# Depthwise convolution of 31 taps: the running sum moved to a PSUM bank, eight taps per tile moved to ScalarE and GpSimd

## The chip, the cores and the metric

The kernel runs on one core of one Trainium2 chip. The metric is the device time of one execution in microseconds (us), measured without the profiler; beside it stands one profiled execution, which the trace describes.

## The reference, cut to what matters

Two transformer blocks in sequence on 512 tokens of 1024 features, in float32. The change lies in the first block, between its first and second feed-forward layers:

```python
u = modulate(x, sh2, sc2)
proj = u @ w_in
xr, gr, conf_in, gate_a, gate_b = jnp.split(proj, IN_SPLITS, axis=-1)

xr = causal_depthwise_conv(xr, rnn_conv_w, rnn_conv_b)          # 4 taps
hr = rg_lru(xr, rglru_w_r, rglru_b_r, rglru_w_i, rglru_b_i, rglru_lambda)
ya = (hr * jax.nn.gelu(gr)) @ rnn_w_proj

glu = conf_in[..., :D_CONV] * jax.nn.sigmoid(conf_in[..., D_CONV:])
hb = causal_depthwise_conv(glu, conf_dw_w, conf_dw_b)           # 31 taps
hb = jax.nn.silu(layer_norm(hb, conf_ln_g, conf_ln_b))
yb = hb @ conf_w_proj

merged = jax.nn.sigmoid(gate_a) * ya + jax.nn.sigmoid(gate_b) * yb
out = merged @ mix_w_out
```

The convolution of 31 taps works on each feature by itself, along the tokens, and looks only backwards. The second block has, among other layers, an attention with a decay (retention), which is named below because it shares a pool of banks.

## The kernel before, in words

Activations lie feature-major: a tile is 128 features by 512 tokens, and eight tiles (KT = 8) make 1024 features. A matrix product of 1024 by 1024 is eight jobs, one for each tile of the result. A job has eight pairs of tiles, and each pair takes three matmuls of 128x512, since values and weights are each split in a high part and a low remainder (`passes`): 24 matmuls that add up in one PSUM bank from the pool `ps`. The weight of a job comes by a DMA that SyncE issues (`wr`, four buffers); ScalarE rounds it to the high part (`wh`, three buffers), and VectorE subtracts to get the low part (`wl`, three buffers). `ft(..., evac, pump)` lays down one job and, behind it, the evacuation of its bank.

PSUM has eight banks of 128x512. `ps` has six of them and `st` two; `st` is for transposes and broadcasts of column statistics.

Work that belongs to no job goes on a list: `later(cost, f)` appends a piece with a cost, and `pump(budget)` takes pieces off the list as jobs are laid down, until their costs use up the budget of the job. `delay(jobs, f)` runs a piece some jobs later, and `settle` empties both lists. The scheduler of the framework then fixes an order for each engine, which the engine keeps; an engine that waits holds up all that stands behind it in its order.

`middle` holds the stage: 16 jobs for the two halves of `conf_in` (`ev_b`, `ev_a`), 16 for `xr` and `gr` with the recurrence behind them, eight each for the two gates, eight of `rnn_w_proj`, then `settle`, eight of `conf_w_proj` and eight of `mix_w_out`. Each `ev_a` makes a tile `g` and puts 30 taps of it on the list; a tap is one VectorE instruction, `hb = g shifted * w + hb`, in place in SBUF. Behind the last tap of a tile follow its sums for the layer norm (`conf_add`), behind the last tile's the column sums by eight transposes (`column_sums`, L280), the power on GpSimd (`rsqrt`, L284), the broadcast by eight more (`diag_bcast`, L273), and then `conf_apply` for each tile: VectorE's corrections, SiLU on ScalarE, the split. The jobs of `conf_w_proj` read what `conf_apply` makes.

Line numbers of the profile that come up below: L133 is any two-operand VectorE or GpSimd operation, L136 any scalar_tensor_tensor (the taps among them, `s<-s,ccw,s`), L147 any ScalarE activation without a bias tile, L152 any matmul of a job.

In the retention of the second block, `ev_g` multiplies a gate job's bank by a tile on VectorE, `scores(h)` takes four banks of `ps` for one head, and the next gate job follows.

Of the kernel before, what the change touches and what calls it, by code (L numbers as in the profile page):

```python
# [9 lines left out]
F32 = mybir.dt.float32  # L10
F32R = mybir.dt.float32r
I32 = mybir.dt.int32
AF = mybir.ActivationFunctionType
ALU = mybir.AluOpType
AX = mybir.AxisListType

S = 512
# [40 lines left out]
class Net:  # L58
    def __init__(self, ctx, tc, a, out):
        self.tc, self.nc, self.a, self.out = tc, tc.nc, a, out  # L60
        pool = lambda **k: ctx.enter_context(tc.tile_pool(**k))
        self.const = pool(name="const", bufs=1)
        self.sl = pool(name="sl", bufs=1)
        self.wr = pool(name="wr", bufs=4)
        self.wh = pool(name="wh", bufs=3)
        self.wl = pool(name="wl", bufs=3)
        self.ps = pool(name="ps", bufs=6, space=bass.MemoryType.PSUM)
        self.st = pool(name="st", bufs=2, space=bass.MemoryType.PSUM)
        self.dr = pool(name="dr", bufs=1, space=bass.MemoryType.DRAM)
        self.stage = ExitStack()  # L70
        self.ar = self.stage.enter_context(tc.tile_pool(name="ar", bufs=AR))
        self.retired = True
        self.n_slots = 61
        self.free = deque(range(self.n_slots))
        self.where = {}
        self.keep = []
        self.uid = 0
        self.items = []
        self.bg = deque()
        self.credit = 0.0  # L80
        self.delayed = []
# [37 lines left out]

    def PS(self):  # L120
        return self.ps.tile([128, S], F32, tag="ps", name=self.name("ps"))

    def ST(self):
        return self.st.tile([128, S], F32, tag="st", name=self.name("st"))
# [477 lines left out]
def first_group(n, xs, X, wg, wu):  # L602


    nc, a = n.nc, n.a
    b1, sh, sc = (n.C([128, 8], name="m1") for _ in range(3))
    at = ADA_AT * 8
    n.ts(b1, n.vecs[:, at + 8:at + 16], 1.0, op0=ALU.add)
    ws, ps, W, raw = [], [], {}, {}
    with_x = [(0, 1), (2, 3, 4), (5, 6, 7), (), (), (), (), ()]  # L610

    def mac(m, k):
        if k == 0:
            ps.append(n.PS() if m < 6 else n.ST())
        hi, lo = ws[m][k // 4]
        c = slice((k % 4) * 128, (k % 4 + 1) * 128)
        n.acc(ps[m], n.passes((hi[:, c], lo[:, c]), X[k]), k == 0, k == KT - 1)

    def fetch(s):
        W[s] = ada_tile(n, KT + s), ada_tile(n, s)  # L620
        n.load(xs[s], a["xT"][s])
        for m in with_x[s]:
            raw[m] = n.wr.tile([128, 1024], F32, tag="wr", name=n.name("wr"))
            n.load(raw[m], (wg, wu)[m % 2][m // 2])

    def modulated(s):
        wsc, wsh = W.pop(s)
        ada_sum(n, wsc, KT + s)
        n.tt(sc[:, s:s + 1], n.mod[:, KT + s:KT + s + 1], b1[:, s:s + 1], ALU.add)
        ada_sum(n, wsh, s)  # L630
        n.tt(sh[:, s:s + 1], n.mod[:, s:s + 1], n.vecs[:, at + s:at + s + 1], ALU.add)
        u = n.A()
        n.act(u, xs[s], AF.Identity, scale=sc[:, s:s + 1], bias=sh[:, s:s + 1])
        X.append(n.split(u))
        n.F(u)

    def weights(s):
        for m in with_x[s]:
            w = raw.pop(m)
            ws.append([n.split(w[:, h * S:(h + 1) * S], lo_eng=(nc.vector, nc.gpsimd)[h]) for h in range(2)])  # L640

    fetch(0)
    fetch(1)
    modulated(0)
    weights(0)
    for s in range(KT):
        if s + 2 < KT:
            fetch(s + 2)
        if s + 1 < KT:
            modulated(s + 1)  # L650
            weights(s + 1)
        for m in range(with_x[s][0] if with_x[s] else 8):
            mac(m, s)
        for m in with_x[s]:
            for k in range(s + 1):
                mac(m, k)
    for t in xs:
        n.act(t, t, AF.Copy, scale=ALPHA)
    n.F(ws)
    return ps  # L660
# [91 lines left out]
            n.load(n.wri[j][h], n.a[w][:, h * S:(h + 1) * S])  # L752


def middle(n, res, X):

    nc, a = n.nc, n.a
    win = a["w_in"]
    st = {}
    hb = {}  # L760
# [9 lines left out]
    def ev_a(m):  # L770
        def evac(ps):
            g = st.pop(("tb", m))
            n.stt(g, g, 1.0, ps, ALU.add, ALU.mult)
            w = lambda k: n.ccw[:, k * 8 + m:k * 8 + m + 1]
            hb[m] = n.A()
            n.act(hb[m], g, AF.Identity, scale=w(30), bias=n.vec("conf_dw_b")[:, m:m + 1])

            def tap(k):
                def f():
                    d = 30 - k  # L780
                    n.stt(hb[m][:, d:], g[:, 0:S - d], w(k), hb[m][:, d:], ALU.mult, ALU.add)
                    if k == 0:
                        n.F(g)
                        n.delay(2, lambda: conf_add(m))
                return f

            for k in range(29, -1, -1):
                n.later(0.63, tap(k))
        return evac

    def conf_add(m):
        conf.add(m)
        if m == KT - 1:
            n.delay(1, conf_stats)
# [87 lines left out]
    w = lambda b, m: win[b * 8 + m]  # L882
# [1021 lines left out]
```

## Time and profile before

| | |
|---|---|
| Time, median of 3 runs | 1859.93 us (1859.61 to 1868.07) |
| Profiled execution | 1861.86 us |
| Its span in the trace | 1860.1 us |
| Mean granted clock of TensorE | 0.988 of full speed |
| TensorE matmul (PE) busy | 1796.9 us, 97% of the span |
| VectorE (DVE) busy | 1250.5 us, 67% |
| ScalarE (ACT) busy | 654.6 us, 35% |
| GpSimd (POOL) busy | 360.4 us, 19% |

The span is the time from the first to the last instruction in the trace; the profiled execution's own time has 1.8 us around it. A busy share is an average over stages that differ: in the stage of the convolution (about 428 to 735 us) VectorE is busy nearly all the time. The duration of an instruction overlaps the next by a little on VectorE, so a rate is read from starts.

### The profile page before, as it was taken

Reading aid. Unit: us, or ns where it says so; the run is one execution under the profiler, and the core shown is the slowest. Engines: PE = TensorE matmul, PEld = TensorE weight load, DVE = VectorE, ACT = ScalarE, POOL = GpSimd, SP = SyncE. Lnnn points to the kernel's source line nnn. Section 1 sums busy time; section 2 is a strip of 40 time slices with the busy share of each in tenths; the row PEclk is TensorE's granted clock in tenths of the full one; section 3 lists DMA queues with packets and bytes.
Section 4 is the critical chain, followed back from the end, with each engine's and each line's share of the span. In section 5 each row is a group of like instructions: output and inputs, shape, how many; then the busy total and the mean of one; then the engine's idle time right before and its main releaser. Section 6 shows DMA issues by size and latency. Waiting matters only on the chain.

```text
span 1860.1 us, 22090 instructions
## 1 busy us (share of the span) xinstructions
PE 1796.9 (97%) x8242; PEld 1480.5 (80%) x8242; DVE 1250.5 (67%) x2242; ACT 654.6 (35%) x891; POOL 360.4 (19%) x316
## 2 busy tenths in 40 slices
PE   5999999999999998999998999999998999999997
PEld 4888888888877887788876888888876778888886
DVE  7888634478999999767443434476599993356644
ACT  4322223333387522424321222334322222354442
POOL 2000001130000000234436963024231010012102
PEclk9999999999999999999999999999998999999999
DMA  8788433233322223235656352454622225653211
GB/s 318 299 318 316 144 111 102 85 119 131 102 80 80 91 94 114 87 129 175 190 151 190 126 198 90 163 173 90 208 70 77 80 86 172 191 158 124 87 46 57
DMA packets 105356, 261.48 MB, mean 141 GB/s; under 512 B 15008, under 2 KB 32032, under 8 KB 105120
## 3 DMA queue, kind: packets, MB, share of 16 engines
q1 hardware_dynamic: 105248, 260.07, 42.6%
q8 instruction: 64, 1.05, 0.2%
q14 instruction: 44, 0.36, 0.1%
HBM read 239.19 MB, written 20.84 MB: 140 GB/s over the span
## 4 chain that ended last, share of the span: by engine, by line
PE 59%; issue 16%; DVE 11%; POOL 6%; DMA 6%; ACT 2%; SPq 1%; DVEq 0%; POOLq 0%; ACTq 0%
PE ps L152 54%; POOL s L133 5%; PE st L152 4%; DVE s L136 3%; DVE wl L133 2%; DVE arr L133 1%; DMA s<-Fd 1%; DVE s L133 1%; DVE st L133 1%; ACT s L147 1%; DMA wr<-in_ffn_w_gate 1%; DMA s<-in_s_bt_im 1%; DVE s L1464 1%; SPq L130 1%; DMA s<-in_s_bt_re 1%
## 5 line engine op out<-in xcount | busy, mean ns | idle before, releaser
L152 PE MATMUL ps<-s,wh 128*128 128x512 f32 (+1 forms) x4272 | 1321.0, 391 | 9.8 <-ACT wh L147 4.9
L152 PEld LDWEIGHTS ps<-s,wh 128*128 128x128 f32 x4272 | 800.5, 189 | 180.1 <-ACT wh L147 7.1
L152 PE MATMUL ps<-s,wl 128*128 128x512 f32 (+1 forms) x2136 | 830.6, 389 | 2.7 <-DVE wl L133 2.7
L147 ACT ACTIVATE wh<-wr 128x1024 fp32r<-128x1024 f32 (+1 forms) x277 | 289.5, 1047 | 834.1 <-PE ps L152 523.8
L133 DVE TENSOR_TENSOR wl<-wr,wh 128x1024 fp32r<-128x1024 f32 (+1 forms) x277 | 357.8, 1292 | 202.1 <-ACT wh L147 199.0
L152 PEld LDWEIGHTS ps<-s,wl 128*128 128x128 f32 x2136 | 402.3, 188 | 87.4 <-DVE wl L133 4.5
L133 POOL TENSOR_TENSOR s<-s,s 128x512 f32<-128x512 f32 (+2 forms) x168 | 232.6, 1389 | 708.0 <-DVE s L136 347.0
L133 DVE TENSOR_TENSOR s<-s,s 128x512 fp32r<-128x512 f32 (+3 forms) x249 | 199.3, 809 | 54.1 <-ACT s L147 52.5
L147 ACT ACTIVATE s<-s 128x512 fp32r<-128x512 f32 (+3 forms) x246 | 153.5, 637 | 224.7 <-DVE s L133 135.4
L152 PE MATMUL ps<-s,s 128*128 128x512 f32 (+7 forms) x648 | 152.5, 386 | 27.8 <-ACT s L147 19.3
L136 DVE SCALAR_TENSOR_TENSOR s<-s,ccw,s 128x503 f32<-128x503 f32 (+27 forms) x240 | 163.2, 735 | 0.7
L152 PEld LDWEIGHTS ps<-s,s 128*128 128x128 f32 (+2 forms) x648 | 108.4, 179 | 66.1 <-issue 22.7
L133 DVE TENSOR_TENSOR s<-s,ps 128x512 f32<-128x512 f32 (+1 forms) x61 | 40.7, 669 | 139.8 <-PE ps L152 139.6
L136 DVE SCALAR_TENSOR_TENSOR s<-ps,c,s 128x512 f32<-128x512 f32 x56 | 41.9, 748 | 83.5 <-PE ps L152 83.2
L389 DVE SCALAR_TENSOR_TENSOR ar<-ar,silc 128x1024 f32<-128x1024 f32 x72 | 89.2, 1251 | 10.2 <-DMA ar<-in_ada_w 9.7
L147 ACT ACTIVATE s<-ps 128x512 f32<-128x512 f32 (+1 forms) x115 | 66.2, 586 | 10.4 <-PE ps L152 10.3
L133 DVE TENSOR_TENSOR arr<-arr,st 128x64 f32<-128x64 f32 x254 | 63.2, 249 | 3.8
L133 DVE TENSOR_TENSOR s<-ps,s 128x512 f32<-128x512 f32 (+4 forms) x80 | 46.6, 615 | 24.6 <-PE ps L152 24.3
L133 DVE TENSOR_TENSOR s<-s,st 128x512 f32<-128x512 f32 x73 | 46.6, 680 | 14.4 <-PE st L273 13.9
L133 DVE TENSOR_TENSOR st<-arr,a 128x64 f32<-128x64 f32 x254 | 52.5, 245 | 3.6
L284 POOL TENSOR_TENSOR ls<-ls,mhalf 128x4 f32<-128x4 f32 x4 | 4.1, 1024 | 257.3 <-DVE ls L136 257.3
L133 POOL TENSOR_TENSOR s<-s 128x256 f32<-128x256 f32 x1 | 0.8, 846 | 246.8 <-ACT s L147 246.8
(155 smaller groups left out, 954.1 us busy)
## 6 DMA issues: line engine op xcount, KB each, us to landing
wr<-in_w_in SPq DMA_DIRECT2D x80, 512.0 KB
ar<-in_ada_w SPq DMA_DIRECT2D x72, 512.0 KB
wr<-in_ffn_w_gate SPq DMA_DIRECT2D x44, 512.0 KB
wr<-in_ffn_w_up SPq DMA_DIRECT2D x44, 512.0 KB
wr<-in_ffn_w_down SPq DMA_DIRECT2D x32, 512.0 KB
s<-Cd SPq DMA_DIRECT2D x32, 256.0 KB
wr<-in_w_out SPq DMA_DIRECT2D x16, 512.0 KB
wr<-in_ffn_w_down SPq DMA_DIRECT2D x16, 384.0 KB
```

Of the source, the lines that this page charges most:

```text
L130: self.nc.sync.dma_start(out=out, in_=in_)
L133: (eng or self.nc.vector).tensor_tensor(out=out, in0=a, in1=b, op=op)
L136: self.nc.vector.scalar_tensor_tensor(out=out, in0=a, scalar=s, in1=b, op0=op0, op1=op1)
L147: self.nc.scalar.activation(out=out, in_=in_, func=f, scale=scale)
L152: self.nc.tensor.matmul(out, lhsT=lhsT, rhs=rhs, start=start, stop=stop)
L284: self.nc.gpsimd.tensor_tensor(out=out, in0=v, in1=self.mhalf[:, 0:n], op=ALU.pow)
L389: n.nc.vector.scalar_tensor_tensor(out=w, in0=w, scalar=1.0, in1=n.silc, op0=ALU.mult, op1=ALU.mult, accum_out=n.mod[:, j:j + 1])
L1464: nc.vector.tensor_copy(out=s[b * 32:(b + 1) * 32], in_=ps[(b ^ 1) * 32:((b ^ 1) + 1) * 32])
```

## The change

The sum of a tile, `acc`, now lies in PSUM, in a bank of its own from a new pool `cv` with one buffer; `ps` gives up one bank, and has five. `begin` sets column 0 of the bank to zero on VectorE and lets ScalarE write the tap with shift 1 into it. VectorE adds the taps 28 to 8 into the bank, 21 in a row. The other eight are products on ScalarE (a scaled copy into an SBUF tile) that GpSimd adds to `h2` in SBUF, where the tap without shift and the bias already are. `end` adds the bank to `h2` on VectorE. The costs on the list are 0.75 for a tap (0.63 before), 0.7 for `end`, 0 for `begin` and the products. Of 240 VectorE taps 168 stay; there are 72 more ScalarE instructions, 64 more on GpSimd, and 16 more on VectorE (8 additions, 8 memsets). `first_group` at the start of the block, which used six `ps` banks and two `st`, takes the `cv` bank as its sixth.

```diff
-        self.ps = pool(name="ps", bufs=6, space=bass.MemoryType.PSUM)
+        self.ps = pool(name="ps", bufs=5, space=bass.MemoryType.PSUM)
+        self.cv = pool(name="cv", bufs=1, space=bass.MemoryType.PSUM)
...
-            ps.append(n.PS() if m < 6 else n.ST())
+            ps.append(n.PS() if m < 5 else n.CV() if m == 5 else n.ST())
...
+POOL_TAPS = 8
...
-            hb[m] = n.A()
-            n.act(hb[m], g, AF.Identity, scale=w(30), bias=n.vec("conf_dw_b")[:, m:m + 1])
+            h2, acc = n.A(), n.CV()
+            n.act(h2, g, AF.Identity, scale=w(30), bias=n.vec("conf_dw_b")[:, m:m + 1])
+
+            def begin():
+                nc.vector.memset(acc[:, 0:1], 0.0)
+                n.act(acc[:, 1:], g[:, 0:S - 1], AF.Copy, scale=w(29))
+
+            def pool_tap(k):
+                def f():
+                    p, d = n.A(), 30 - k
+                    n.act(p[:, d:], g[:, 0:S - d], AF.Copy, scale=w(k))
+                    n.tt(h2[:, d:], h2[:, d:], p[:, d:], ALU.add, nc.gpsimd)
+                    n.F(p)
+                return f
 
             def tap(k):
                 def f():
                     d = 30 - k
-                    n.stt(hb[m][:, d:], g[:, 0:S - d], w(k), hb[m][:, d:], ALU.mult, ALU.add)
-                    if k == 0:
-                        n.F(g)
-                        n.delay(2, lambda: conf_add(m))
+                    n.stt(acc[:, d:], g[:, 0:S - d], w(k), acc[:, d:], ALU.mult, ALU.add)
                 return f
 
-            for k in range(29, -1, -1):
-                n.later(0.63, tap(k))
+            def end():
+                hb[m] = h2
+                n.tt(h2, h2, acc, ALU.add)
+                n.F(g)
+                n.delay(2, lambda: conf_add(m))
+
+            n.later(0.0, begin)
+            mine, others = range(28, POOL_TAPS - 1, -1), list(range(POOL_TAPS - 1, -1, -1))
+            for i, k in enumerate(mine):
+                n.later(0.75, tap(k))
+                if i % 2 == 0 and others:
+                    n.later(0.0, pool_tap(others.pop(0)))
+            n.later(0.7, end)
```

The new lines move line numbers: L133, L136, L147 and L152 of before are L137, L140, L151 and L156 after.

First place: TensorE's order at the end of the `rnn_w_proj` jobs. `ps_5414` is the bank of the last of these jobs, `st_5467` and `st_5473` take the column sums' transposes, and `st_5484` is the broadcast. Before:

```order
L152 MATMUL ps_5414<-s_4714,wh_5331 128x512
L152 MATMUL ps_5414<-s_4713,wl_5332 128x512
L280 MATMUL st_5467<-ident_86,s_3907 128x128 [waits DVE_49,PE_49]
L280 MATMUL st_5467<-ident_86,s_3907 128x128 x3
L280 MATMUL st_5473<-ident_86,s_3862 128x128 [waits DVE_49]
L280 MATMUL st_5473<-ident_86,s_3862 128x128 x3
L273 MATMUL st_5484<-ident_86,ls_5466 128x128 [waits Pool_49]
L273 MATMUL st_5484<-ident_86,ls_5466 128x128 x3
L273 MATMUL st_5489<-ident_86,ls_5466 128x128 [waits DVE_49,PE_49]
```

After the change the last of these jobs is `ps_5613`, the one ahead of it `ps_5563`; the column sums are `st_5590` and `st_5596`, the broadcast `st_5639`:

```order
L156 MATMUL ps_5563<-s_4833,wl_5487 128x512
L284 MATMUL st_5590<-ident_89,s_3896 128x128 [waits PE_49]
L284 MATMUL st_5590<-ident_89,s_3896 128x128 x3
L284 MATMUL st_5596<-ident_89,s_3849 128x128 x4
L156 MATMUL ps_5613<-s_4152,wh_5522 128x512 [waits Activation_49]
L156 MATMUL ps_5613<-s_4153,wh_5522 128x512
...
L156 MATMUL ps_5613<-s_4833,wl_5523 128x512
L277 MATMUL st_5639<-ident_89,ls_5589 128x128 [waits Pool_49]
L277 MATMUL st_5639<-ident_89,ls_5589 128x128 x3
```

The column sums' transposes have moved ahead of the last job's 24 matmuls; the broadcast still stands behind them.

Second place: VectorE's order where the first tiles' taps are under way. `s590` and `s600` are the sums of two tiles, `ccw` the taps' weights, `wl` a weight's low part. Before:

```order
L136 SCALAR_TENSOR_TENSOR s600_3227<-s595_3189,ccw499_2788,s600_3227 128x511 [waits Activation_49]
L136 SCALAR_TENSOR_TENSOR s590_3151<-s585_3117,ccw499_2788,s590_3151 128x498 [waits DVE_49]
L136 SCALAR_TENSOR_TENSOR s600_3227<-s595_3189,ccw499_2788,s600_3227 128x510 [waits DVE_49]
L136 SCALAR_TENSOR_TENSOR s590_3151<-s585_3117,ccw499_2788,s590_3151 128x497 [waits DVE_49]
L136 SCALAR_TENSOR_TENSOR s600_3227<-s595_3189,ccw499_2788,s600_3227 128x509 [waits DVE_49]
L136 SCALAR_TENSOR_TENSOR s590_3151<-s585_3117,ccw499_2788,s590_3151 128x496 [waits DVE_49]
```

After the change, where tile 0 (`cv591`) ends and tile 1 (`cv605`) begins:

```order
L140 SCALAR_TENSOR_TENSOR cv591_3155<-s585_3120,ccw499_2791,cv591_3155 128x490 [waits DVE_49]
L137 TENSOR_TENSOR s590_3154<-s590_3154,cv591_3155 128x512 [waits DVE_49,Pool_49]
L786 MEMSET cv605_3241 128x1 [waits DVE_49]
L140 SCALAR_TENSOR_TENSOR cv605_3241<-s598_3200,ccw499_2791,cv605_3241 128x510 [waits Activation_49]
L140 SCALAR_TENSOR_TENSOR cv605_3241<-s598_3200,ccw499_2791,cv605_3241 128x509 [waits DVE_49]
L137 TENSOR_TENSOR wl629_3376<-wr627_3373,wh628_3375 128x1024 [waits DMAHW5_49,PE_49,Activation_49]
```

Taps of two tiles stood in turn; now one tile's taps stand in a row, and the next tile's first tap follows the closing addition, the memset and ScalarE's product.

Third place: ScalarE's order in the stage of the recurrence. `wh` is a weight's split, `s<-s,ccw` a product for GpSimd. Before, three successive splits:

```order
L147 ACTIVATE wh856_4795<-wr855_4793 128x1024 [waits DMAHW5_49,DVE_49,PE_49]
L147 ACTIVATE s854_4786<-ps853_4761 128x512 [waits PE_49]
L147 ACTIVATE wh861_4833<-wr860_4831 128x1024 [waits DMAHW6_49,DVE_49,PE_49]
L147 ACTIVATE s859_4824<-ps858_4799 128x512 [waits PE_49]
L147 ACTIVATE wh866_4871<-wr865_4869 128x1024 [waits DMAHW7_49,DVE_49,PE_49]
```

After the change, from one split (`wh894`) to the next (`wh901`):

```order
L151 ACTIVATE wh894_4839<-wr893_4837 128x1024 [waits DMAHW3_49,PE_49]
L151 ACTIVATE s890_4825<-ps889_4800 128x512 [waits PE_49]
L151 ACTIVATE s946_5178<-s667_3619,ccw499_2791 128x486 [waits DVE_49]
L151 ACTIVATE s948_5188<-s667_3619,ccw499_2791 128x484 [waits Pool_49]
L151 ACTIVATE s954_5226<-s667_3619,ccw499_2791 128x483 [waits Pool_49]
L151 ACTIVATE s966_5310<-s679_3699,ccw499_2791 128x489 [waits Pool_49]
L151 ACTIVATE s972_5352<-s679_3699,ccw499_2791 128x487 [waits Pool_49]
L151 ACTIVATE s978_5394<-s679_3699,ccw499_2791 128x486 [waits Pool_49]
L151 ACTIVATE s979_5399<-s679_3699,ccw499_2791 128x485 [waits Pool_49]
L151 ACTIVATE s897_4868<-ps896_4843 128x512 [waits PE_49]
L151 ACTIVATE wh901_4885<-wr900_4883 128x1024 [waits DMAHW4_49]
```

Between two splits there was one evacuation of a bank; now up to seven products stand there too, six of which wait for GpSimd (`Pool_49`).

In the second block TensorE's order is the same as before. The first matmul of the gate job behind the four score matmuls waited for ScalarE (`[waits Activation_49]`, the split of its weight); after the change it waits for VectorE (`[waits DVE_49]`), whose instruction there reads the bank that the tile now gets.

## Rows read from the trace of the kernel before

**Rows 1.** Busy us of PE, PEld, DVE, ACT, POOL by stretch, then clock

```profile
512.00:620.00 108.00, 108.00 (x446) 83.43 (x445) 108.00 (x163) 86.77 (x106) 0.00 (x0) 1.00 0.25 83
...
620.00:728.00 108.00, 108.00 (x478) 89.48 (x477) 107.72 (x153) 35.19 (x44) 0.00 (x0) 1.00 0.28 93
...
740.00:752.00 12.00, 4.75 (x14) 3.56 (x15) 9.79 (x20) 4.58 (x7) 1.02 (x1) 0.61 0.21 79
...
1406.00:1412.00 6.00, 4.16 (x11) 3.30 (x12) 5.73 (x20) 0.00 (x0) 1.22 (x2) 0.72 0.25 85
```

**Rows 2.** What TensorE waited for, 416 to 870 us

```profile
PE st L273 <- POOL ls L284: 6.6, 2, 6.1
...
PE ps L152 <- ACT s L147: 3.2, 1, 3.2
```

**Rows 3.** The order of time, 721 to 750 us (start, duration, engine)

```profile
722.65 0.61 PE L152 MATMUL ps<-s,wh 128*128 128x512 f32 x2
...
723.33 0.61 PE L152 MATMUL ps<-s,wh 128*128 128x512 f32 x2
...
726.02 1.06 ACT L147 ACTIVATE wh<-wr 128x1024 fp32r<-128x1024 f32 x1 [4.33 <-PE ps L152]
...
727.34 1.22 DVE L133 TENSOR_TENSOR wl<-wr,wh 128x1024 fp32r<-128x1024 f32 x1
...
736.93 1.03 PE L280 MATMUL st<-ident,s 128*128 128x128 f32 x8
...
740.01 1.28 DVE L281 TENSOR_REDUCE ls<-st 128x4 f32<-128x512 f32 x2
...
742.98 1.02 POOL L284 TENSOR_TENSOR ls<-ls,mhalf 128x4 f32<-128x4 f32 x1 [247.43 <-DVE ls L136]
...
744.05 1.97 PE L273 MATMUL st<-ident,ls 128*128 128x128 f32 x8 [6.08 <-POOL ls L284]
...
749.22 1.72 PE L152 MATMUL ps<-s,wh 128*128 128x512 f32 x3 [3.20 <-ACT s L147]
```

**Rows 4.** VectorE in the order of time, 430 to 447 us

```profile
430.38 4.66 DVE L136 SCALAR_TENSOR_TENSOR s<-s,ccw,s 128x511 f32<-128x511 f32 x6
...
442.25 4.66 DVE L136 SCALAR_TENSOR_TENSOR s<-s,ccw,s 128x499 f32<-128x499 f32 x7
```

**Rows 5.** Groups of instructions on VectorE by line and shape, 416 to 737 us

```profile
L133 DVE TENSOR_TENSOR wl<-wr,wh 128x1024 fp32r<-128x1024 f32 x57 | 70.2, 1231 | 4.6 <-ACT wh L147 4.5
...
L133 DVE TENSOR_TENSOR s<-s,s 128x512 f32<-128x512 f32 x46 | 31.0, 685 | 0.1
```

**Rows 6.** The same, VectorE and GpSimd, 880 to 1040 us

```profile
L133 DVE TENSOR_TENSOR wl<-wr,wh 128x1024 fp32r<-128x1024 f32 x27 | 39.6, 1465 | 70.5 <-ACT wh L147 70.1 <-DMA s<-in_s_bt_im 0.2
...
L133 DVE TENSOR_TENSOR s<-s,ps 128x512 f32<-128x512 f32 x10 | 6.9, 687 | 24.6 <-PE ps L152 24.6
...
L133 POOL TENSOR_TENSOR s<-s,s 128x512 f32<-128x512 f32 x48 | 71.9, 1512 | 87.1 <-DMA s<-Fd 69.8 <-DMA s<-in_s_bt_re 8.7 <-DMA s<-in_s_bt_im 4.6
```

**Rows 7.** The same, VectorE, 1200 to 1300 us

```profile
L133 DVE TENSOR_TENSOR s<-s,s 128x512 f32<-128x512 f32 x17 | 15.6, 936 | 0.2
```

**Rows 8.** The page's costliest groups: taps, and an addition that reads PSUM

```profile
L136 DVE SCALAR_TENSOR_TENSOR s<-s,ccw,s 128x503 f32<-128x503 f32 (+27 forms) x240 | 163.2, 735 | 0.7
...
L136 DVE SCALAR_TENSOR_TENSOR s<-ps,c,s 128x512 f32<-128x512 f32 x56 | 41.9, 748 | 83.5 <-PE ps L152 83.2
```

**Rows 9.** Groups on ScalarE, whole span: a scaled copy of 512 columns

```profile
L147 ACT ACTIVATE s<-ps,rs 128x512 f32<-128x512 f32 x8 | 5.5, 684 | 3.7 <-PE ps L152 3.7
```

**Rows 10.** The order of time in the second block, 1407 to 1440 us

```profile
1407.84 0.19 PEld L152 LDWEIGHTS ps<-wl,s 128*128 128x128 f32 x1 [2.75 <-DVE wl L133]
...
1427.86 0.73 PE L152 MATMUL ps<-s,wh 128*128 128x512 f32 x2
...
1438.41 0.68 DVE L133 TENSOR_TENSOR s<-ps,s 128x512 f32<-128x512 f32 x1
...
1439.98 4.60 PE L152 MATMUL ps<-s,s 128*128 128x512 f32 x8 [6.38 <-DVE s L133]
```

More of the change, by code (lines that the diff above doesn't have):

```diff
@@ L121, in PS, with CV @@
         return self.ps.tile([128, S], F32, tag="ps", name=self.name("ps"))
+    def CV(self):
+        return self.cv.tile([128, S], F32, tag="cv", name=self.name("cv"))
     def ST(self):
```

## Prediction

> **What bounds the kernel now.** I began with the engines' busy time by stretch. TensorE and VectorE are both full over the convolution's 300 us (108.00 of 108 us on each from 512 to 620, 108.00 and 107.72 from 620 to 728), at a granted clock of 1.00 [rows 1]. Two full engines leave open which one sets the pace, so the waits of TensorE come next: between 416 and 870 us it waits for no tap and no weight, only for one GpSimd result (6.1 us) and then for ScalarE (3.2 us) [rows 2]. So VectorE is full but keeps up, and taps taken from it shorten nothing while TensorE is fed. What the taps do set is the one hole at their end, which I read in the order of time [rows 3]: the eight transposes of the column sums run at 736.93, right behind the last rnn_w_proj job; two reductions (740.01, 1.28 us) and the power on GpSimd (742.98, 1.02 us) follow; the broadcast starts at 744.05 after 6.08 us of idle TensorE, and the first conf_w_proj matmul at 749.22 after 3.20 us more. In 740 to 752 us TensorE works 4.75 of 12 us at a granted clock of 0.61 [rows 1]. With 5.17 us from broadcast to matmul, of which the broadcast itself takes 1.97, this hole costs about 12 us (749.22 less 737.96, the end of the column sums, and what the lower clock takes): the most that this edit can win.
>
> **The change, part by part.** *Hole, -6.1 us.* The second cut of the change shows the column sums one job earlier. A job is 24 matmuls, three per 0.68 us [rows 3], so 5.44 us. The sums then start near 731.5, and the chain behind them needs 1.28 + 1.02 us and three VectorE steps between 742.34 and 742.98 (0.64 us), some 3 us that now lie under the last job. The broadcast follows that job's end at 737.96 in place of 744.05: -6.1. The 5.17 us behind it (VectorE's corrections, SiLU, split) stay. The part reaches -12 only if they close too, and 0 if VectorE finishes its taps a job late. The sums need the last tile by 731.5, 5.4 us sooner than before.
>
> *VectorE's own sum.* 72 taps go. Taps of two tiles in turn start 0.653 us apart ((4.66 - 0.74) / 6), taps that each need the one before 0.78 us ((4.66 - 0.75) / 5) [rows 4]. So -72 x 0.653 = -47.0 us. One CV bank allows one tile at a time: of the 168 that stay, 104 stand right behind another tap of their tile in the new order (second place of the change), +104 x 0.13 = +13.5. Eight closing additions of 0.685 us [rows 5], less 0.09 overlap: +4.8; eight one-column memsets: near nothing. At tiles 1 to 3 the first tap follows memset and ScalarE's product at once, about 1.3 us each by the 0.684 us copy [rows 9] and a launch: +4. Net -25 us of 300.
>
> *What that spare can't do.* It can't be saved up. The split of a weight begins when TensorE has let go of the buffer three weights back: at 726.02 it had waited 4.33 us for that, and its low part ended at 728.56 [rows 3]. Two jobs are 10.88 us, so a weight is ready at most 8.3 us ahead. Two places of the new order ask for more.
>
> First, between two low parts of rnn_conv time (wl823 and wl872, for jobs near 612 and 639) VectorE now has 55 instructions: scans, gate arithmetic, 15 taps. At the rate of the stretch 512 to 620, 163 in 108.00 us or 0.663 each [rows 1], that is 36.5 us, for five jobs of 27.2: 9.3 against 8.3 of lead, a wait of 1.0. Here GpSimd's additions also stand densest. What they cost VectorE: a low part means 1231 ns where GpSimd is idle [rows 5] and 1465 with its 71.9 us of additions in 160 us [rows 6]; an addition of two SBUF tiles 685 [rows 5] and 936 [rows 7]. With some 25 such instructions and 5 low parts, 25 x 0.25 + 5 x 0.23 = 7.4 us if each meets one, 0 if none; I take 2, since the new order spreads the additions beyond this stretch. Together 3 us.
>
> Second, ScalarE. Its list (third place of the change) has six products that each wait for GpSimd, ahead of the split wh901. Between wh878 and wh901 stand 17 products, and an addition takes 1.51 us [rows 6]: 25.7 us for three jobs of 16.3. That is 9.4 behind against 8.3 ahead: 1.1 us, with the low part behind it 2. A wait of 2.33 us came with a granted clock of 0.72, 11 matmuls taking 4.16 us [rows 1, 10] for 2.5 at 0.227 each, so 1.7 us more; I add 1 for the two waits. Sum of this part +6, bounds 0 (no additions met, ScalarE never behind) and 17.
>
> *Taps on PSUM.* No row shows VectorE writing PSUM. Reading it is free: 748 ns beside 735 for taps that are 16 columns shorter on average [rows 8], and 687 for an addition with one PSUM input [rows 6] beside 685 with none [rows 5]. Bounds: 0, and once more the 0.13 us that a dependent tap waits now, 168 x 0.13 = 21.8 us. The rows on reading are the nearest, so I take 0.03 each: 5 us, which the spare of 25 covers outside the two places.
>
> [...]
>
> GpSimd and VectorE: an addition with a PSUM input keeps 687 ns in the very stretch where the low parts lengthen to 1465 [rows 6]. I therefore charge contention to no tap.
>
> [...]
>
> *One PSUM bank less, +4.7 us.* The ps pool serves the whole program. In the second block the gate job, four score matmuls and the next gate job hold six ps tiles. With five the sixth reuses the gate job's bank, and the order shows it: its first matmul waited for ScalarE's split and now waits for VectorE. The reader of that bank (ev_g's multiplication) ran at 1438.41 for 0.68 us, since VectorE was busy with state steps; the matmul ran at 1427.86 [rows 10]. So TensorE now stands until 1439.1, then does the 5.44 us job, then the values that before started at 1439.98 after 6.38 us idle. Before, the job filled part of that gap; now it comes after: 1439.1 + 5.44 - 1439.98 = +4.6, with a hand-over 4.7. Bounds 0 (VectorE reaches the reader as soon as TensorE stops) and 7 (a lower clock over a longer pause). The other reuses find their bank read in time or lose under 2 us ahead of this stop, which absorbs them.
>
> **Sum.** -6.1 + 6 + 4.7 = +4.6. The profiled execution took 1861.86 us, so 1866.5; it stands 1.93 above the median of the runs (1859.93), so I predict 1864.5.
>
> **The rivals.** (1) *The waits at 612 to 655 stay away.* VectorE loses 25 us of work, which speaks for it; against it, the spare is capped at 8.3 us. Then -6.1 + 4.7 = -1.4: 1858.5. (2) *PSUM writes are slow* (ends on the other side of no change). A dependent tap waits for its write into the bank. At 0.1 us a tap, 16.8 us: 10 above the 5 that I assumed absorbed, and VectorE, not TensorE, sets the pace through the convolution: 1864.5 + 10 = 1874.5. It decides from about 0.03 us above my value, where 168 x 0.03 = 5 us are no longer covered and the sum passes 9.3 us. Against it is only that reading costs nothing. (3) *The bank costs nothing,* because VectorE's queue in front of the reader moves up: 1859.8. (4) *The whole hole closes* and nothing else is lost: 1859.93 - 12 = 1848. It needs the corrections behind the broadcast to run ahead of the matmuls, and they follow it by 5.17 us in any order.
>
> **How the numbers follow.** 0.5% (9.3 us) is about what a measurement of this kernel tells from no change. Forecast, 1860 to 1869: 0.44. Rival 1: 0.18. Rival 2: 0.28. Rival 3: 0.06. Rival 4: 0.04. The forecast, rivals 1 and 3 end within 0.5%; 0.02 of the forecast falls beyond the upper edge: same 0.66, slower 0.30, faster 0.04. The range 1856 to 1877 runs from below rival 1 to the bound of 17 for the waits (1864.5 + 11 = 1875.5), and leaves out rival 4 and the worst of rival 2.
>
> **What would show it.** Right: the broadcast directly behind the last rnn_w_proj job with no wait for the power on GpSimd; short waits of TensorE for weight splits between 610 and 660 us; a TensorE wait of about 11 us for VectorE in the second block where 6.38 stood; tap groups near 735 ns with a start distance under 0.82. Wrong: tap distances of 0.85 and more with VectorE full and TensorE waiting again and again from 440 us on (rival 2); no waits before the hole (rival 1); a second-block stop unchanged at 6 us (rival 3).

## The result, and the profile after

The changed kernel takes 1874.57 us (median of 8 runs, 1871.86 to 1879.47) and the kernel before 1860.57 (8 runs). The ratio is 1.0073, with a 95% interval of 1.006 to 1.0086: slower by 0.73%. The profiled execution took 1873.04 us, its span is 1871.0: 10.9 longer than before.

What TensorE waited for between 400 and 890 us after the change (engine, line, releaser; us in total, times, longest) answers to [rows 2]:

```profile
PE ps L156 <- DVE wl L137: 7.8, 5, 2.8
PE ps L156 <- ACT s L151: 5.1, 1, 5.1
PE ps L156 <- DVE s L140: 1.4, 1, 1.4
...
PE st L277 <- POOL ls L288: 0.5, 1, 0.5
PE ps L156 <- ACT wh L151: 0.3, 1, 0.3
```

The wait for the power on GpSimd (L288) has gone from 6.1 to 0.5. In its place stand 7.8 us in five waits for weight remainders (`wl`). Four of them, 7.0 us between 632 and 663, are new; the fifth, 0.8 at 880, stood at 873 before too. With 1.4 us for a tile of the recurrence (`DVE s`) and 0.3 for a split (`ACT wh`) TensorE waits 8.7 us in the convolution's stage, where it had no wait before.

By stretch (busy PE, PEld, DVE, ACT, POOL, granted clock, DMA): first two stretches after the change, to be read against [rows 1], then 600 to 662 us before and after:

```profile
512.00:620.00 108.00, 106.57 (x441) 82.32 (x440) 107.65 (x152) 91.40 (x114) 21.09 (x11) 1.00 0.22 74
620.00:728.00 108.00, 100.60 (x430) 81.01 (x429) 103.36 (x126) 50.52 (x72) 39.84 (x25) 0.98 0.26 87
```

```profile
600.00:662.00 62.00, 62.00 (x271) 50.60 (x271) 62.00 (x91) 34.90 (x45) 0.00 (x0) 1.00 0.29 94
```

```profile
600.00:662.00 62.00, 53.74 (x220) 41.55 (x218) 59.17 (x68) 44.12 (x62) 35.74 (x22) 0.97 0.20 68
```

TensorE loses little until 620, and then works only 100.60 of 108 us. In 600 to 662 it is idle for 8.3 us, and its 220 matmuls take 53.74 us, 0.244 each beside 0.229 before: 3.4 us more, at a granted clock of 0.97 beside 1.00. The place is the second half of the recurrence, where the prediction put its two waits.

VectorE's instructions by shape in 600 to 662 us, first before and then after (count, busy, mean ns):

```profile
L133 DVE TENSOR_TENSOR wl<-wr,wh 128x1024 fp32r<-128x1024 f32 x11 | 13.4, 1220 | 0.0
L133 DVE TENSOR_TENSOR s<-s,s 128x512 f32<-128x512 f32 x14 | 9.3, 682 | 0.0
L136 DVE SCALAR_TENSOR_TENSOR s<-s,s 128x512 f32<-128x512 f32 x7 | 4.8, 682 | 0.0
...
L133 DVE TENSOR_TENSOR s<-s,s 128x512 fp32r<-128x512 f32 x4 | 2.7, 682 | 0.0
L143 DVE TENSOR_SCALAR s<-s 128x512 f32<-128x512 f32 x5 | 2.1, 412 | 0.0
```

```profile
L137 DVE TENSOR_TENSOR wl<-wr,wh 128x1024 fp32r<-128x1024 f32 x9 | 13.2, 1469 | 2.6 <-ACT wh L151 2.6
L137 DVE TENSOR_TENSOR s<-s,s 128x512 f32<-128x512 f32 x11 | 10.8, 987 | 0.0
L140 DVE SCALAR_TENSOR_TENSOR s<-s,s 128x512 f32<-128x512 f32 x6 | 6.6, 1094 | 0.0
L137 DVE TENSOR_TENSOR s<-s,s 128x512 fp32r<-128x512 f32 x4 | 4.2, 1050 | 0.0
...
L147 DVE TENSOR_SCALAR s<-s 128x512 f32<-128x512 f32 x5 | 3.5, 703 | 0.0
```

The same shapes take 0.25 to 0.41 us longer each on the mean. Counted with the numbers after, these five alone cost 9 x 0.249 + 11 x 0.305 + 6 x 0.412 + 4 x 0.368 + 5 x 0.291 = 11.0 us more VectorE time in 62.

What one meeting costs stands in the order of time after the change:

```profile
645.15 5.20 POOL L137 TENSOR_TENSOR s<-s,s 128x483 f32<-128x483 f32 x3 [0.25 <-ACT s L151]
...
649.28 1.62 DVE L137 TENSOR_TENSOR s<-s,s 128x512 f32<-128x512 f32 x1
...
651.47 0.68 DVE L137 TENSOR_TENSOR s<-s,s 128x512 f32<-128x512 f32 x1
...
653.03 7.13 POOL L137 TENSOR_TENSOR s<-s,s 128x486 f32<-128x486 f32 x5 [2.68 <-ACT s L151]
653.87 4.66 DVE L140 SCALAR_TENSOR_TENSOR cv<-s,ccw,cv 128x508 f32<-128x508 f32 x6
...
657.67 0.70 ACT L151 ACTIVATE s<-s,ccw 128x486 f32<-128x486 f32 x1 [1.90 <-POOL s L137]
...
661.15 1.23 DVE L137 TENSOR_TENSOR wl<-wr,wh 128x1024 fp32r<-128x1024 f32 x1 [2.62 <-ACT wh L151]
```

VectorE's addition at 649.28 meets additions of GpSimd and takes 1.62 us; the one at 651.47 falls into a pause of GpSimd and takes 0.68. The six taps at 653.87 run beside additions all the while, and yet start (4.66 - 0.75) / 5 = 0.78 us apart, as dependent taps do without them [rows 4]. The last two rows show a second route to a late weight: ScalarE's product waited 1.90 us for GpSimd, the split behind it (660.07) came late, and the remainder waited 2.62 us for that split. TensorE lost 0.28 + 0.53 = 0.8 of its 8.7 us that way.

The hole, in the order of time (start, duration), answers to [rows 3]:

```profile
744.19 1.03 PE L284 MATMUL st<-ident,s 128*128 128x128 f32 x8
...
747.97 1.02 POOL L288 TENSOR_TENSOR ls<-ls,mhalf 128x4 f32<-128x4 f32 x1 [43.94 <-DVE ls L140]
...
750.52 1.04 PE L277 MATMUL st<-ident,ls 128*128 128x128 f32 x8
751.51 0.62 DVE L145 TENSOR_SCALAR s<-s,vecs 128x256 f32<-128x256 f32 x2 [1.10 <-DMA s<-in_memT]
...
752.64 4.27 DVE L137 TENSOR_TENSOR s<-s,st 128x512 f32<-128x512 f32 x7
...
756.64 1.72 PE L156 MATMUL ps<-s,wh 128*128 128x512 f32 x3 [5.08 <-ACT s L151]
```

The column sums run a job earlier, the broadcast directly behind the last rnn_w_proj job, and the power on GpSimd lies under that job, as forecast. From the column sums to the first conf_w_proj matmul it was 749.22 - 736.93 = 12.29 us; now it is 756.64 - 744.19 = 12.45, of which 5.44 is the job that stands between. The hole gave back 5.3 us. The missing 0.8 of the forecast 6.1 is in the row at 751.51: VectorE waited 1.10 us there for a small load (`in_memT`), so its corrections start 2.12 us behind the broadcast, not 1.16 (745.21 less 744.05 before).

The column sums stand 744.19 + 5.44 - 736.93 = 12.7 us later in TensorE's work than before. That is what the convolution's stage lost: 8.7 us of waits, 3.4 of slower matmuls, and 0.6 that I have not placed.

The taps themselves, where no addition of GpSimd is under way:

```profile
486.28 3.88 DVE L140 SCALAR_TENSOR_TENSOR cv<-s,ccw,cv 128x506 f32<-128x506 f32 x5
```

Five dependent taps on the bank take 3.88 us: (3.88 - 0.75) / 4 = 0.78 from start to start, the same as dependent taps in SBUF [rows 4]. VectorE's writing into PSUM costs nothing beyond that.

The second block, beside [rows 10]:

```profile
1446.16 0.68 DVE L137 TENSOR_TENSOR s<-ps,s 128x512 f32<-128x512 f32 x1
...
1446.90 1.22 PE L156 MATMUL ps<-s,wh 128*128 128x512 f32 x2 [11.18 <-DVE s L137]
```

The gate job waits 11.18 us for the reader of its bank (1446.16, 0.68 us), as forecast. In all: +12.7 in the convolution, -5.3 in the hole, and 3.5 that are left of the span's 10.9 for the second block and the rest. These are two single executions; the medians differ by 14.0, and the traces do not say where the other 3 us lie.

### The profile page after: what moved, and what is told of

It reads as the page before. It is cut to its first block, busy times and chain, and to the rows that moved or that the text cites. A ratio compares the mean times of both kernels' runs of the same rounds, so it can differ in the third digit from the quotient of the medians.

```text
span 1871.0 us, 22229 instructions
## 1 busy us (share of the span) xinstructions
PE 1797.3 (96%) x8242; PEld 1478.1 (79%) x8242; DVE 1241.2 (66%) x2186; ACT 697.2 (37%) x963; POOL 462.4 (25%) x380
## 4 chain that ended last, share of the span: by engine, by line
PE 69%; DVE 17%; DMA 5%; POOL 3%; issue 3%; ACT 2%; SPq 1%; DVEq 0%; POOLq 0%; ACTq 0%
PE ps L156 65%; PE st L156 4%; DVE wl L137 3%; DVE s L137 3%; POOL s L137 3%; DVE s L140 2%; DVE cv L140 2%; DVE arr L137 1%; DVE st L137 1%; ACT s L151 1%; DMA s<-in_s_bt_re 1%; DMA s<-Fd 1%; SPq L134 1%; DVE s L147 1%; DVE s L1491 1%
## 5 line engine op out<-in xcount | busy, mean ns | idle before, releaser
L156 PE MATMUL ps<-s,wh 128*128 128x512 f32 (+1 forms) x4272 | 1323.4, 391 | 23.1 <-DVE s L137 11.9
L156 PEld LDWEIGHTS ps<-s,wh 128*128 128x128 f32 x4272 | 801.1, 189 | 195.0 <-DVE s L137 13.4
L156 PE MATMUL ps<-s,wl 128*128 128x512 f32 (+1 forms) x2136 | 832.1, 390 | 9.5 <-DVE wl L137 9.4
L151 ACT ACTIVATE wh<-wr 128x1024 fp32r<-128x1024 f32 (+1 forms) x277 | 289.2, 1046 | 796.4 <-PE ps L156 507.5
L137 POOL TENSOR_TENSOR s<-s,s 128x512 f32<-128x512 f32 (+7 forms) x232 | 334.6, 1446 | 818.3 <-ACT s L151 362.0
L137 DVE TENSOR_TENSOR wl<-wr,wh 128x1024 fp32r<-128x1024 f32 (+1 forms) x277 | 364.7, 1317 | 198.4 <-ACT wh L151 186.7
L156 PEld LDWEIGHTS ps<-s,wl 128*128 128x128 f32 x2136 | 402.7, 189 | 97.1 <-DVE wl L137 14.1
L137 DVE TENSOR_TENSOR s<-s,s 128x512 fp32r<-128x512 f32 (+3 forms) x249 | 204.6, 829 | 54.1 <-ACT s L151 52.3
L151 ACT ACTIVATE s<-s 128x512 fp32r<-128x512 f32 (+3 forms) x246 | 153.5, 637 | 186.9 <-DVE s L137 99.8
L156 PE MATMUL ps<-s,s 128*128 128x512 f32 (+8 forms) x624 | 145.2, 382 | 22.8 <-ACT s L151 19.1
L156 PEld LDWEIGHTS ps<-s,s 128*128 128x128 f32 (+2 forms) x624 | 102.7, 177 | 59.1 <-ACT s L151 21.3
L137 DVE TENSOR_TENSOR s<-s,ps 128x512 f32<-128x512 f32 (+1 forms) x60 | 40.1, 668 | 140.0 <-PE ps L156 140.0
L140 DVE SCALAR_TENSOR_TENSOR cv<-s,ccw,cv 128x510 f32<-128x510 f32 (+6 forms) x168 | 124.3, 740 | 5.9 <-ACT cv L151 2.3
L140 DVE SCALAR_TENSOR_TENSOR s<-ps,c,s 128x512 f32<-128x512 f32 x56 | 41.9, 748 | 83.9 <-PE ps L156 83.6
L151 ACT ACTIVATE s<-ps 128x512 f32<-128x512 f32 (+1 forms) x115 | 66.3, 587 | 13.3 <-PE ps L156 13.2
L137 DVE TENSOR_TENSOR arr<-arr,st 128x64 f32<-128x64 f32 x254 | 63.2, 249 | 3.8
L137 DVE TENSOR_TENSOR s<-ps,s 128x512 f32<-128x512 f32 (+4 forms) x80 | 46.7, 616 | 25.8 <-PE ps L156 25.5
L137 POOL TENSOR_TENSOR s<-s 128x256 f32<-128x256 f32 x1 | 0.8, 846 | 246.9 <-ACT s L151 246.9
L137 DVE TENSOR_TENSOR s<-s,st 128x512 f32<-128x512 f32 x73 | 46.6, 681 | 13.3 <-PE st L277 12.9
L137 DVE TENSOR_TENSOR st<-arr,a 128x64 f32<-128x64 f32 x254 | 52.6, 245 | 3.6
L151 ACT ACTIVATE s<-s,ccw 128x487 f32<-128x487 f32 (+6 forms) x64 | 41.2, 691 | 34.7 <-DVE cv L140 18.7
```

The source lines that it names most:

```text
L137: (eng or self.nc.vector).tensor_tensor(out=out, in0=a, in1=b, op=op)
L140: self.nc.vector.scalar_tensor_tensor(out=out, in0=a, scalar=s, in1=b, op0=op0, op1=op1)
L151: self.nc.scalar.activation(out=out, in_=in_, func=f, scale=scale)
L156: self.nc.tensor.matmul(out, lhsT=lhsT, rhs=rhs, start=start, stop=stop)
```

## The experiments

Two theories of the 12.7 us stand against each other, and a third that the prediction had as a rival. **C**: GpSimd's additions read SBUF, and VectorE's instructions with two SBUF inputs get longer beside them (the addition from 682 to 987 ns on the mean, above). **Q**: ScalarE's products wait for GpSimd and hold up the weight splits behind them. **P**: taps are slow because their sum lies in PSUM. The bank that the jobs lost is a matter of its own.

**e1_bank_only: the kernel before, with one bank less for the jobs.**

```diff
-        self.ps = pool(name="ps", bufs=6, space=bass.MemoryType.PSUM)
+        self.ps = pool(name="ps", bufs=5, space=bass.MemoryType.PSUM)
+        self.cv = pool(name="cv", bufs=1, space=bass.MemoryType.PSUM)
...
-            ps.append(n.PS() if m < 6 else n.ST())
+            ps.append(n.PS() if m < 5 else n.CV() if m == 5 else n.ST())
```

> Kernel before with nothing changed but the split of PSUM: five banks for the jobs, one bank set aside (used once, by the first group). Theory (a bank less makes the gate job behind the four score matmuls wait for the reader of its bank): TensorE's wait near 1428 us grows from 6.4 to about 11.2 us, the profile is 3 to 5 us longer than before (about 1865), nothing else moves. Rival (the bank costs nothing, the later shift in the changed kernel comes from somewhere else): the wait stays at 6.4 us, time as before.

It took 1867.74 us, ratio 1.0034 (1.0021 to 1.0047). TensorE's longest wait between 1400 and 1470 us:

```profile
PE ps L156 <- DVE s L137: 11.2, 1, 11.2
```

This is the wait of the changed kernel, with no other part of the change. By the medians the bank costs 6.2 us of time, by the interval 3.9 to 8.7. The profiled execution, 1870.82 us, is 9.0 longer than that of the kernel before, where I had expected 3 to 5.

**e2_six_banks: the changed kernel, with the bank handed back behind `middle`.**

```diff
     def PS(self):
+        self.turn = (self.turn + 1) % 6
+        if self.six and self.turn == 5:
+            return self.CV()
         return self.ps.tile([128, S], F32, tag="ps", name=self.name("ps"))
...
     n.do(lambda: n.F(HB))
+    n.do(lambda: setattr(n, "six", True))
```

> Changed kernel, but behind the convolution's stage every sixth bank of a job is the sum's bank, so that jobs have six again. Theory of the bank: the 11.2 us wait goes back to about 6.4, the profile is 3 to 5 us shorter than the changed kernel's (about 1869 by the profiled execution); waits between 610 and 665 us stay. Rival (bank costs nothing): time as the changed kernel.

It took 1868.12 us, ratio 1.0038 (1.0024 to 1.0051), beside 1.0073 for the changed kernel: 0.35%, about 6.5 us, less; its profiled execution 1865.05, 8 less (3 to 5 expected). Its wait in the second block, and below it its waits for weights between 416 and 760:

```profile
PE ps L160 <- DVE s L141: 6.4, 1, 6.4
```

```profile
PE ps L160 <- DVE wl L141: 5.4, 4, 2.8
...
PE ps L160 <- ACT wh L155: 1.9, 1, 1.9
```

The stop in the second block is back at 6.4. In the convolution's stage, where this edit changes nothing, all waits stay: 5.4 and 1.9 us here, and again 1.4 for the tile of the recurrence, make the same 8.7. The two runs on the bank agree from both sides: 6.2 us more and 6.5 less.

**e3_no_adds: the products are made, GpSimd's additions left out.** The sum lacks the eight taps.

```diff
                     n.act(p[:, d:], g[:, 0:S - d], AF.Copy, scale=w(k))
-                    n.tt(h2[:, d:], h2[:, d:], p[:, d:], ALU.add, nc.gpsimd)
                     n.F(p)
```

> Changed kernel without GpSimd's 64 additions: the eight products of a tile are still made by ScalarE, but are left out of the sum. Theory C (GpSimd's reads of SBUF lengthen VectorE's weight remainders and gate arithmetic): in 600 to 662 us the remainder falls from 1469 to about 1225 ns, the two-input additions from 987 to about 685, TensorE's waits there go, the profile is about 12 us shorter (1861). Theory Q (ScalarE's products wait for GpSimd and hold up the splits): the same time, so this run alone does not tell C from Q. Theory P (taps in PSUM are slow): waits stay, time as the changed kernel.

It took 1861.09 us, ratio 1.0000 (0.999 to 1.0011). All of TensorE's waits between 416 and 760 us, and VectorE's two-input additions in 600 to 662:

```profile
PE ps L156 <- ACT s L151: 4.3, 1, 4.3
```

```profile
L137 DVE TENSOR_TENSOR s<-s,s 128x512 f32<-128x512 f32 x15 | 10.1, 693 | 0.1
```

Nothing is left but the wait behind the broadcast. All of VectorE's 168 taps still write PSUM here, so P is out. What remains are the shorter hole, about 5 us less, and the lost bank, about 6 us more, and the ratio of 1.0000 fits that. This run takes away the additions and the waits for them at once, so it does not tell C from Q.

**e4_pool_writes: each addition replaced by three memsets.** GpSimd stays busy and ScalarE's products still wait for it, but it reads nothing; the sum lacks the eight taps. The scheduler moved some splits ahead by two products.

```diff
-                    n.tt(h2[:, d:], h2[:, d:], p[:, d:], ALU.add, nc.gpsimd)
+                    for _ in range(3):
+                        nc.gpsimd.memset(p[:, d:], 0.0)
```

> Changed kernel in which each of GpSimd's 64 additions is replaced by three memsets of the product's tile, about 0.53 us each by the rows of the kernel before, so 1.6 us of GpSimd work that writes SBUF and reads none; the products are left out of the sum. ScalarE's products still wait for GpSimd. Theory C (it is the reads): VectorE's durations in 600 to 662 us fall to those of the kernel before (1220 and 685 ns), waits of TensorE there fall to 3 us or less, the profile is 9 to 12 us shorter than the changed kernel. Theory Q (pace of ScalarE's list): waits of 8 us and more stay, the profile within 3 us of the changed kernel. Theory P: as the changed kernel.

It took 1862.31 us, ratio 1.0005 (0.9995 to 1.0016). The stretch 600 to 662 us, two shapes of VectorE in it, and all of TensorE's waits between 416 and 760:

```profile
600.00:662.00 62.00, 62.00 (x271) 50.64 (x270) 59.89 (x85) 49.29 (x70) 38.31 (x81) 1.00 0.26 90
```

```profile
L137 DVE TENSOR_TENSOR s<-s,s 128x512 f32<-128x512 f32 x14 | 9.6, 688 | 0.1
...
L147 DVE TENSOR_SCALAR s<-s 128x512 f32<-128x512 f32 x4 | 2.2, 551 | 0.0
```

```profile
PE ps L156 <- ACT s L151: 5.1, 1, 5.1
```

GpSimd works 38.31 of 62 us here (the changed kernel's additions take 35.7 there), and no weight is late. VectorE's additions are back at 688 ns. Only the TENSOR_SCALAR, with one input and an output in SBUF, stays longer, 551 beside 412. So what lengthened the instructions with two inputs (987 ns for the addition in the changed kernel) is GpSimd's reading, not its being busy. ScalarE's products wait 4.4 us for GpSimd in this stretch, beside 2.9 in the changed kernel, and VectorE waits 1.4 us for splits, but TensorE for nothing: the pace that GpSimd sets on ScalarE's list does not by itself make TensorE wait. Q is out as the main cause, as far as the moved splits allow to say; the 0.8 us above that went its way came on top of C.

In 600 to 662 us the addition of two SBUF tiles means 987 ns beside GpSimd's additions (the changed kernel), 688 beside its memsets and 693 where it is idle (e3). TENSOR_SCALAR, with one SBUF input, was longer beside reads (703 ns) and beside writes (551). The next run puts the taps to the same test.

**e5_sbuf_sum: the changed kernel, with the sum in SBUF in place of the bank.** (The bank stays unused in this stage.)

```diff
-            h2, acc = n.A(), n.CV()
+            h2, acc = n.A(), n.A()
...
                 n.tt(h2, h2, acc, ALU.add)
-                n.F(g)
+                n.F(g, acc)
```

> Changed kernel with the running sum of the 21 taps in an SBUF tile in place of the PSUM bank (five banks for the jobs stay, one is unused); taps of two tiles then stand in turn again. Theory C (GpSimd's reads lengthen VectorE instructions with two SBUF inputs, not those with one): the taps rise from 740 ns to 900 and more while additions run, the waits of TensorE between 430 and 730 us grow from 9 to 15 us or more, time 5 to 20 us above the changed kernel (1880 to 1895). Rival (it does not matter where the sum lies): within 4 us of the changed kernel, with the gain of taps in turn, 0.13 us each for some 100 of them, at most 13 us faster.

It took 1918.33 us, ratio 1.0311 (1.0295 to 1.0326): 44 us above the changed kernel, where I had expected 20 at most. The taps in the changed kernel between 416 and 760 us, then in this one between 416 and 790, and its waits for weight remainders:

```profile
L140 DVE SCALAR_TENSOR_TENSOR cv<-s,ccw,cv 128x510 f32<-128x510 f32 (+6 forms) x168 | 124.3, 740 | 5.9 <-ACT cv L151 2.3
```

```profile
L140 DVE SCALAR_TENSOR_TENSOR s<-s,ccw,s 128x502 f32<-128x502 f32 (+18 forms) x168 | 156.1, 978 | 0.7 <-ACT s L151 0.2
```

```profile
PE ps L156 <- DVE wl L137: 35.5, 10, 7.4
```

The tap goes from 740 to 978 ns, 168 x 0.24 = 40 us more on VectorE, and 35.5 us of waits for remainders follow. With GpSimd adding beside it, the PSUM bank is what makes this change bearable.

**e6_cost_055 and e7_cost_053: the kernel before, with the tap's cost on the list lowered.** This moves column sums (0.55), and the broadcast too (0.53), up in TensorE's order; no work leaves VectorE.

```diff
-                n.later(0.63, tap(k))
+                n.later(0.55, tap(k))
```

> Kernel before with one number changed: the cost of a tap on the list is 0.55 in place of 0.63, which puts the column sums one job earlier in TensorE's order, as the change did; no tap leaves VectorE. Theory H (the hole closes by the place of the column sums alone; VectorE has 8.3 us of lead to give): TensorE's wait for the power on GpSimd (6.1 us) goes, time 5 to 7 us below the kernel before (about 1855). Rival (VectorE is full, so the column sums come no earlier or the weights late): waits of 4 us and more for weight remainders or for the column sums' input, time within 2 us of the kernel before or above.

> The same with 0.53: the broadcast too then stands inside the last rnn_w_proj job. Theory H: the wait for ScalarE behind the broadcast (3.2 us) shrinks as well, 6 to 11 us below the kernel before. Rival (VectorE's lead is used up): TensorE waits for the column sums' input or weight remainders take it back, within 3 us of the run with 0.55 or above it.

The first took 1862.10 us, ratio 1.0006 (0.9997 to 1.0016), the second 1858.87, ratio 0.9987 (0.9978 to 0.9996). In the first, the two waits at the hole, and what stands around the column sums:

```profile
PE st L280 <- DVE s L133: 4.8, 1, 4.8
PE ps L152 <- ACT s L147: 3.8, 1, 3.8
```

```profile
734.19 2.08 DVE L133 TENSOR_TENSOR s<-s,s 128x512 f32<-128x512 f32 x3
...
735.75 1.94 PE L280 MATMUL st<-ident,s 128*128 128x128 f32 x8 [4.82 <-DVE s L133]
```

The transposes start at 735.75, among the last three additions for the layer norm, after 4.8 us of waiting: most of the 6.1 us that went came back as this wait. The theory that the place of the sums closes the hole alone is wrong: VectorE has to be done a job sooner. In the second, VectorE does the taps first and the remainders late (its two longest sums of waits):

```profile
PE ps L152 <- DVE wl L133: 4.0, 3, 2.0
PE ps L152 <- ACT s L147: 1.3, 1, 1.3
```

It gains 2 us of the 6 to 11 expected: the wait for ScalarE is down to 1.3, but 4.0 us of waits for remainders are new. The lead of 8.3 us buys little; VectorE needs less work.

**e8_early_tiles: products for GpSimd only in tiles 0 to 3, all taps of the others in the bank, six banks, cost 0.60.**

```diff
-            mine, others = range(28, POOL_TAPS - 1, -1), list(range(POOL_TAPS - 1, -1, -1))
+            pt = POOL_TAPS if m < 4 else 0
+            mine, others = range(28, pt - 1, -1), list(range(pt - 1, -1, -1))
...
-                n.later(0.75, tap(k))
+                n.later(0.60, tap(k))
```

> Changed kernel with six banks for the jobs behind the convolution's stage, products for GpSimd only in the first four tiles (the other four have all their taps on VectorE, in the bank), cost of a tap 0.60. Theory C: no additions while the gate arithmetic runs, so the remainder and the two-input additions in 600 to 662 us are back at 1225 and 685 ns; but VectorE has 32 taps more than in the changed kernel, all dependent, some 25 us, so that its spare is gone: waits of 0 to 10 us in the later part, time 1850 to 1864. Rival (late splits on ScalarE or something else in the stretch is the cause): waits between 610 and 665 us stay at 8 us.

It took 1860.32 us, ratio 1.0000 (0.9991 to 1.001). TensorE's two largest waits between 416 and 800 us:

```profile
PE ps L160 <- ACT s L155: 4.3, 1, 4.3
PE ps L160 <- DVE wl L141: 1.9, 3, 0.9
```

The waits between 610 and 665 are nearly gone (1.9 us in three), as C has it. What is left behind the broadcast is 4.3 us; the next run, whose late tiles take their taps in turn in SBUF, has 1.3 there. In 600 to 662 us the remainder means 1279 ns and the two-input addition 748, not the 1225 and 685 that were expected; e1_bank_only, where GpSimd adds nothing, has 1276 and 742 (see the last section). The profiled execution took 1857.23 us, below the one of before; the timed runs show no difference.

**e9_best_052 and e10_best_056: tiles 0 to 3 as in the changed kernel, tiles 4 to 7 as in the kernel before, six banks.** Costs 0.75 and 0.52, or 0.65 and 0.56; for tiles 0 to 3 the products follow every tap, not every second one.

```diff
+            early = m < 4
-            h2, acc = n.A(), n.CV()
+            h2, acc = n.A(), n.CV() if early else None
...
+            def plain(k):
+                def f():
+                    d = 30 - k
+                    n.stt(h2[:, d:], g[:, 0:S - d], w(k), h2[:, d:], ALU.mult, ALU.add)
+                    if k == 0:
+                        hb[m] = h2
+                        n.F(g)
+                        n.delay(2, lambda: conf_add(m))
+                return f
+
+            if not early:
+                for k in range(29, -1, -1):
+                    n.later(0.52, plain(k))
+                return
```

> Tiles 0 to 3 as in the changed kernel (sum in the bank, eight products for GpSimd, cost 0.75), tiles 4 to 7 as in the kernel before (30 taps in SBUF, cost 0.52), six banks for the jobs behind the convolution's stage. GpSimd's additions then lie ahead of the gate arithmetic and beside taps that keep their sum in PSUM. Theory C: no wait for weight remainders between 520 and 720 us above 2 us in all, and with some 15 us taken from VectorE the column sums and the broadcast come a job earlier: the hole shrinks from 12 to about 2 us, no bank is missed: 7 to 11 us below the kernel before. Rival (VectorE's lead is used up as with cost 0.53 alone): waits of 4 us and more for remainders, within 4 us of the kernel before.

> The same with costs 0.65 (tiles 0 to 3) and 0.56 (tiles 4 to 7), which puts column sums and broadcast elsewhere by a few taps. Theory C: 7 to 12 us below the kernel before, waits of at most 2 us for remainders. Rival: as for the run before it.

They took 1850.28 us, ratio 0.9938 (0.9925 to 0.9952), and 1850.51, ratio 0.9942 (0.9929 to 0.9955): 10 us below the kernel before, 24 below the changed one. Of the first, all of TensorE's waits between 416 and 800 us, and two stretches:

```profile
PE ps L160 <- ACT s L155: 1.3, 1, 1.3
PE ps L160 <- DVE s L141: 0.2, 1, 0.2
```

```profile
428.00:512.00 84.00, 84.00 (x371) 69.22 (x370) 80.78 (x103) 47.31 (x67) 47.23 (x32) 1.00 0.28 95
512.00:620.00 108.00, 108.00 (x448) 83.80 (x447) 108.00 (x163) 91.00 (x111) 2.72 (x1) 1.00 0.24 84
```

GpSimd works 47.23 us ahead of 512 and 2.72 from there to 620, so its additions end before most of the gate arithmetic. TensorE has no wait in the convolution's stage, and of the waits in the hole 1.5 us are left; in the second run it has no wait at all between 416 and 800. These runs change several things at once. The cost alone won 2 of the 10 us (e7); how the rest divides among bank, place of the products and order was not tested.

## Why the prediction was right or wrong

The time fell within the range, which had been drawn as far as the bound of 17 us for the waits, but well above the forecast: 14.0 us over the kernel before where 4.6 was forecast, past the 0.5% that I had called "same" (0.66) into "slower" (0.30). The three terms of the sum were of the right kind, but one measured twice its size. Step by step:

- *What bounds the kernel, and the hole.* Right. VectorE full and not waited for, and the hole as the only thing to win. The hole gave 5.3 of the forecast 6.1; e3, with 4.3 us of wait behind the broadcast, shows that the steps there do not close by themselves. e6 bears out the condition that I had set, that VectorE finish its taps a job sooner: the place of the column sums alone won nothing. VectorE's own sum held as well: without the additions (e3) it is busy for 280.66 us between 428 and 736, beside 306.64 before, 26.0 less where I forecast 25. (Its +4 for the first taps' waits for ScalarE's product was too much: 2.3 us in three waits, in the row of the taps under e5. The launch in the 1.3 us that I took for each was my estimate, no row shows it; each wait was 0.77.)
- *The spare that can't be saved up.* Right in place and kind: short waits for splits and remainders between 610 and 665 us. The term "6, bounds 0 and 17" measured 12.7, of which 8.7 are waits. Without the additions TensorE waits for no weight (e3), so the wait of 1.0 that I charged to VectorE's list alone was not there either. For slower matmuls behind the waits I added 1 us; they cost 3.4.
- *The step that failed* is the 2 us that I took of "25 x 0.25 + 5 x 0.23 = 7.4 us if each meets one". The runs put 11.0 us and more of VectorE's time in its place. The additions crowd just where the gate arithmetic stands, 35.7 us of them in 62, where I argued that they spread beyond it, though I had written that they stand densest here. The 0.25 was a mean over instructions that met an addition and others that met none; here 0.31 and 0.41 came out, and 0.94 for a single one (1.62 beside 0.68). And I had left out TENSOR_SCALAR (412 to 703 ns), which has only one SBUF input.
- *ScalarE's list.* Of the 6 us, 3 were for products ahead of a split. 0.8 of the 8.7 us of waits came that way in the changed kernel, and 1.9 + 0.5 = 2.4 in e2, in both beside lengthened VectorE instructions. In e4, where the products wait longer for GpSimd in 600 to 662, TensorE waits for no weight: this part is no cause by itself, and smaller than I had it.
- *Taps on PSUM.* The 0.03 us per tap was too much: 0.78 from start to start, as in SBUF. The rows that I read for it (748, 687) were the right ones. Rival 2 gave 1874.5, which is what was measured, by a mechanism that these runs rule out; that the numbers meet is chance.
- *Contention charged to no tap.* Right, and worth far more than I knew: 44 us (e5).
- *The bank.* +4.7 forecast at the right place, with the right wait (11.2). In the trace it is 3.5 of the span, by the timed runs 6.2 us (e1) and 6.5 (e2), more than forecast. With the bank handed back (e2) about 7 of the 14.0 us stay, which is the 12.7 of the stage less the 5.3 of the hole.

## What to carry to other kernels

Before handing sums to GpSimd, look at what VectorE does in that stretch: here the instructions with two SBUF inputs got longer beside additions that read SBUF (the addition from 682 to 987 ns on the mean), taps that had one of the two in PSUM did not (0.78 us from start to start with and without), TENSOR_SCALAR with its one input did (412 to 703 ns), and the price of a meeting is read from single instructions that met (0.94 us for one), not from a mean over a stretch (0.25 to 0.41). Work taken from a full engine pays only where something waits for it (in e3 VectorE was busy 26.0 us less, and only the hole got shorter, by about 5 us), and spare time there can't be carried past a buffer that another engine has to free (8.3 us of lead at most here). A bank taken for one stage can be missed in a much later one that shares the pool, as here in the second block (11.2 us of wait in place of 6.4): hand it back.

## What the runs showed that I had not expected

VectorE's recorded durations vary from one execution to the next without its pace changing. In 600 to 662 us the remainder means 1220 ns before and 1276 in e1_bank_only, where this stage is the same program, the two-input addition 682 and 742; VectorE is full and does 91 instructions in both. So a difference of 60 ns in a mean is read from starts before it is believed. The lengthening beside GpSimd shows in the pace too: VectorE does 68 instructions in that stretch after the change, and 87 in e3, where the additions are left out.
